# First adaLN modulation of a hybrid encoder layer: two of its four sum blocks made by one-row TensorE products, x's squares shared by ScalarE and VectorE, and the first token half's products written ahead

## Chip, cores and metric

The kernel runs on one core of a Trainium2 chip. Its time is the device time of one execution in microseconds (us). A run of it takes about 1318 us, and its executions lie within 0.3% of each other. TensorE (PE in the profile) multiplies matrices into PSUM; VectorE (DVE), ScalarE (ACT) and GpSimd (POOL) work on tiles element by element; SyncE (SP) issues all transfers. Every engine works off its own list of instructions in order, and the engines wait for each other by semaphores.

## The reference, cut to what matters

The layer is a residual block of two sub-layers. The change lies in the first lines:

```python
mod = jnp.dot(jax.nn.silu(c), w_ada[l]) + b_ada[l]          # c: (1, 1024), w_ada: (1024, 6*1024)
sh_a, sc_a, g_a, sh_m, sc_m, g_m = jnp.split(mod, N_MOD, axis=-1)
h = modulate(rmsnorm(x, g_attn_norm[l]), sh_a, sc_a)        # rmsnorm(x)*g*(1+sc_a) + sh_a, x: (1, 1024, 1024)
proj = jnp.dot(h, w_in[l])                                  # split into latents, rotary key and q, k, v
# two attentions (latent attention, chunked band attention), output projection, gated residual,
# then a second modulated norm, a gated MLP with a causal convolution, gated residual
```

Only `sh_a` and `sc_a` (two times 1024 numbers, each a sum over 1024 rows of `w_ada`) and the squares of `rmsnorm(x)` are computed in another way by the change. The results are the same but for rounding.

## The kernel before, in words

All data is float32. A product that needs full accuracy is made of three products of rounded parts (`gemm3`, L154 to L156: high by high, high by low, low by high). `x` is held as eight blocks of 128 tokens (`x0` to `x7`, in the listing of instructions x_112 to x_126 by even numbers), and the 1024 channels as eight groups d of 128. Tokens come in two halves h of 512.

The first stage (up to about 70 us) goes so:

- **Squares.** For each block of x, ScalarE squares it and sums it along the row (L224), GpSimd turns the sum into 1/sqrt(mean) by two small operations (L119, L120), and VectorE scales the block by it (L226).
- **Modulation sums.** `w_ada` for shift and scale comes as four blocks dd of 512 columns (two channel groups d each), each in four transfers of 512 KB (`adaw`, L209) with five buffers for all of them. `ada_pair(dd)` sums a block: VectorE multiplies the eight 128-row slices by one column of silu(c) each and adds them up in `adacc` (L276 for the first, L278 for the other seven). That leaves 128 partial sums for each column, and TensorE adds them over the partitions by multiplying with ones (`p_ada`, L293). Three small VectorE operations (L296 to L298) make the scale and the shift of channel group d, `modT`.
- **Pages.** For each d and h, TensorE transposes four blocks of x (`ht_ps`, L233, one PSUM bank for each h), and `mod_transpose` applies scale and shift. The rounded high part `hT` is written by ScalarE (L236). The exact value `hv` is written by ScalarE for h = 0 (L239) and VectorE for h = 1 (L241). The low part is the difference, made by GpSimd for h = 0 and VectorE for h = 1 (both L242).
- **Products.** For each d, 24 products of 256 columns add to the first query and key projection `qk` (eight token blocks, three products each). After d = 7 ScalarE reads the sums (L349), and the next projection (`ipv`) and the first attention follow.
- **Weights.** The first value projection's weights (`wv_r`, eight transfers of L258, issued behind the last `adaw`) are split while d = 4 to 7 are worked on: high part by VectorE (L81), low part by GpSimd (L84), squares by VectorE (L267).

The loop over d calls `ada_pair(dd + 1)` at each even d ahead of its own pages, so VectorE's sums for the next block are written between the pages of this one. The order in which instructions stand on each engine is not that of the code alone: a scheduler that runs over the whole program places each instruction where it expects it to become ready. Transfers are all issued by SyncE in one list; a transfer into a buffer that is still read holds up those behind it.

After the first stage come the band attention (to about 340 us), the latent attention (to about 600 us), the output projection and the MLP (to the end).

Of the kernel before, what the change touches and what calls it, by code (L numbers as in the profile page):

```python
# [13 lines left out]
F32 = mybir.dt.float32  # L14
# [50 lines left out]
def layer_kernel(ctx, tc, I, out):  # L65
# [155 lines left out]
    for t in range(NT):  # L221
        xt = xs[t]
        junk = st.tile([P, D], mybir.dt.bfloat16, name=f"xj{t}", tag="hv", bufs=2)
        act.activation(junk[:], xt[:], AF.Square, accum_out=ssx[:, t:t + 1])  # L224
        rsqrt_mean(rx[:, t:t + 1], ssx[:, t:t + 1], D)
        dve.tensor_scalar(xt[:], xt[:], rx[:, t:t + 1], None, op0=MUL)  # L226
# [34 lines left out]
    def wv0_split(k):  # L261
        w = hw.tile([P, 2, 256], F32R, name=f"wv0_s{k}", tag="ws", bufs=16)
        junk = st.tile([P, 512], F32, name=f"wv0_j{k}", tag="wvj", bufs=1)
        with tc.issue_after(anchor["lov"]), tc.issue_after(anchor["lop"]):
            hi_of("v", w[:, 0], wv0r[k][:])
            lo_of("p", w[:, 1], wv0r[k][:], w[:, 0])
            dve.tensor_tensor_reduce(junk[:, :256], wv0r[k][:], wv0r[k][:], 1.0, 0.0, MUL, ADD,  # L267
                                     accum_out=ssw0[:, k:k + 1])
        wv0.append((w[:, 0], w[:, 1]))

    def ada_pair(dd):
        acc = rtile(f"adacc_{dd}")
        for k in range(ND):
# [5 lines left out]
        accs[dd] = acc  # L279

    ada_pair(0)
    for d in range(ND):
        dd, half = divmod(d, 2)
        if half == 0 and dd + 1 < ND // 2:
            for c in range(4):
                load_ada(dd + 1, c)
            if dd + 2 == ND // 2:
                wv0_load()
            ada_pair(dd + 1)
        pt = ps.tile([P, 512], F32, name=f"p_ada{d}", tag="mm", bufs=2)  # L290
        for i in range(2):
            c0 = half * 256 + i * P
            pe.matmul(pt[:, i:i + 1], accs[dd][:, c0:c0 + P], ones[:, 0:1], start=True, stop=True)  # L293

# [3 lines left out]
        dve.tensor_tensor(modT[:, 1, d:d + 1], pt[:, 1:2], pk[:, C_B + d:C_B + d + 1], op=ADD)  # L298
        for h in range(2):
            hT[d, h] = mod_transpose(lambda j: xs[4 * h + j][:, d * P:(d + 1) * P], d, h, 0, ps, ("T", "pv")[h], 1,  # L300
                                     hw, "hT", st, 16, "v" if h else "a", "v" if h else "p")
# [3 lines left out]
        for t in range(NT):  # L305
            h, j = divmod(t, 4)
            sl = slice(j * P, (j + 1) * P)
            gemm3(qk0[h][:, j * 256:(j + 1) * 256],
                  [(hT[d, h][:, 0, sl], hT[d, h][:, 1, sl]) + wqk[d]], start=(d == 0 and j % 2 == 0), stop=(d == ND - 1 and j % 2 == 1))
# [1350 lines left out]
```

## Time and profile before

| | |
|---|---|
| median of three runs | 1318.42 us (1316.21 to 1319.64) |
| the profiled execution | 1320.49 us, its span 1318.7 us |
| mean granted TensorE clock | 0.964 |
| busy: PE, DVE, ACT, POOL | 1192.2, 1080.2, 627.3, 597.4 us |
| instructions | 18701 |

The page has a line for each engine's busy time and the span in 40 slices. The views used below are the timeline (start, duration, engine, line, operation, and in brackets the idle time before it and what ended it), tables of busy time in chosen stretches, the waits in a stretch, and the instructions of one line or tile. A duration of a pipelined TensorE product is longer than the step to the next one.

### The profile page before, as it was taken

The numbers are of one execution on the slowest core, as the hardware profiler recorded it, in microseconds if no ns is written. First come the engines' busy times: TensorE is split into PE (matmuls) and PEld (weight loads), VectorE is DVE, ScalarE is ACT, GpSimd is POOL, SyncE is SP. The second block draws the span as 40 slices with busy tenths as digits, with TensorE's granted clock in tenths as the row PEclk, the third lists the DMA queues.
The fourth block names the chain that finished last, engine by engine and source line by source line (L and its number), as shares of the span: only waits on it lengthen the run. The fifth ranks groups of instructions, "written<-read, shape, count | busy, mean of one in ns | idle before, by whom it ended". The sixth has DMA issues, their size and how long they took to land. (4 is left out here: it accounts for less than half of the span.)

```text
span 1318.7 us, 18701 instructions
## 1 busy us (share of the span) xinstructions
PE 1192.2 (90%) x6168; PEld 993.5 (75%) x6168; DVE 1080.2 (82%) x1864; ACT 627.3 (48%) x1148; POOL 597.4 (45%) x629
## 2 busy tenths in 40 slices
PE   4899889988768987868899999999999999999998
PEld 3789889878546766756777888888888886888886
DVE  6979988887589988874789888888889887687667
ACT  5455654455656454542375444443444444433331
POOL 5485773586687643454616444554444431000000
PEclk9999898989879899989999999999999999999999
DMA  8416768665233687789602334333343337943441
GB/s 326 144 55 153 170 146 187 157 161 119 48 85 62 148 165 155 146 173 300 265 17 84 125 104 136 112 114 125 93 131 106 128 104 245 394 145 109 128 160 64
DMA packets 223690, 190.83 MB, mean 145 GB/s; under 512 B 148709, under 2 KB 166373, under 8 KB 223593
## 3 DMA queue, kind: packets, MB, share of 16 engines
q1 hardware_dynamic: 223592, 189.64, 50.5%
q8 instruction: 48, 0.79, 0.2%
q14 instruction: 50, 0.40, 0.1%
HBM read 117.50 MB, written 37.49 MB: 118 GB/s over the span
## 5 line engine op out<-in xcount | busy, mean ns | idle before, releaser
L77 ACT ACTIVATE dnP<-dnr 128x1024 fp32r<-128x1024 f32 x73 | 77.5, 1064 | 116.1 <-PE dnA_P L1471 46.4
L1443 DVE TENSOR_TENSOR dnP<-dnr,dnP 128x1024 fp32r<-128x1024 f32 x72 | 88.7, 1236 | 51.8 <-ACT dnP L77 51.7
L73 POOL TENSOR_SCALAR hlm<-Pm,rim 128x512 f16<-128x512 f32 (+3 forms) x96 | 67.9, 716 | 66.7 <-issue 22.5
L84 POOL TENSOR_TENSOR wf<-wu,wf 128x512 fp32r<-128x512 f32 x22 | 38.6, 1752 | 116.6 <-ACT wf L77 116.6
L84 POOL TENSOR_TENSOR wb<-wu,wb 128x512 fp32r<-128x512 f32 x22 | 44.9, 2040 | 84.5 <-ACT wb L77 56.9
L1305 DVE SCALAR_TENSOR_TENSOR u<-c,cvp,u 128x1023 f32<-128x1023 f32 x44 | 55.8, 1310 | 27.6 <-ACT u L1304 24.8
L855 DVE SCALAR_TENSOR_TENSOR hlm<-Pm,rim,hlm 128x512 f16<-128x512 f32 (+3 forms) x96 | 68.7, 728 | 6.4 <-POOL hlm L73 6.2
L73 POOL TENSOR_SCALAR hlc<-Pc,ric 128x640 f16<-128x640 f32 (+2 forms) x64 | 49.7, 780 | 47.3 <-DVE ric L836 18.4
L833 ACT ACTIVATE Pc<-sc,mc 128x640 f32<-128x640 f32 (+2 forms) x64 | 42.3, 661 | 54.3 <-DVE mc L822 37.2
L833 ACT ACTIVATE Pm<-sm,mm 128x128 f32<-128x128 f32 (+3 forms) x64 | 47.2, 737 | 37.3 <-DVE mm L826 20.0
L895 PE MATMUL pvm<-PTm,vt 128*128 128x256 f16 (+1 forms) x320 | 43.6, 284 | 22.6 <-DMA PTm<-hlm 21.6
L1304 ACT ACTIVATE u<-c,cvp 128x1024 f32<-128x1024 f32 x44 | 52.4, 1238 | 23.6 <-DVE c L1403 16.7
L895 PEld LDWEIGHTS <-vt 128*128 128x128 f16 x320 | 31.3, 105 | 35.9 <-DMA PTm<-hlm 15.8
L855 DVE SCALAR_TENSOR_TENSOR hlc<-Pc,ric,hlc 128x640 f16<-128x640 f32 (+2 forms) x64 | 51.3, 806 | 8.4 <-POOL hlc L73 8.2
L77 ACT ACTIVATE wc<-ws 128x512 fp32r<-128x512 f32 x21 | 13.3, 632 | 93.1 <-DVE ws L1153 87.2
L154 PE MATMUL ipq<-wq_s,hT 128*128 128x256 f32 x192 | 56.4, 294 | 0.0
L1306 DVE SCALAR_TENSOR_TENSOR u<-c,cvp,u 128x1022 f32<-128x1022 f32 x44 | 55.5, 1301 | 0.0
L155 PE MATMUL ipq<-wq_s,hT 128*128 128x256 f32 x192 | 55.0, 287 | 0.0
L156 PE MATMUL ipq<-wq_s,hT 128*128 128x256 f32 x192 | 55.0, 287 | 0.0
L1470 PE MATMUL dnA_P<-dnP 128*128 128x512 f32 x132 | 51.3, 389 | 0.0
L1471 PE MATMUL dnA_P<-dnP 128*128 128x512 f32 x132 | 51.3, 389 | 0.0
L1469 PE MATMUL dnA_P<-dnP 128*128 128x512 f32 x132 | 51.2, 389 | 0.0
(441 smaller groups left out, 4420.5 us busy)
## 6 DMA issues: line engine op xcount, KB each, us to landing
wu<-w_up SPq DMA_DIRECT2D x44, 512.0 KB, 3.6
dnr<-g_d SPq DMA_DIRECT2D x73, 256.0 KB, 2.7
aw<-w_ada SPq DMA_DIRECT2D x48, 256.0 KB, 3.2
g_d<-u SPq DMA_DIRECT2D x22, 512.0 KB, 3.0
dnr<-w_down SPq DMA_DIRECT2D x44, 256.0 KB, 5.4
adaw<-w_ada_a SPq DMA_DIRECT2D x16, 512.0 KB, 6.2
x<-x SPq DMA_DIRECT2D x16, 512.0 KB, 9.4
g_d<-gs SPq DMA_DIRECT2D x22, 256.0 KB, 2.8
```

Of the source, the lines that this page charges most:

```text
L73: pool.tensor_scalar(o, i, s, 1.0, op0=MUL, op1=MUL)
L77: act.activation(o, i, AF.Copy)
L84: (pool if eng == "p" else dve).tensor_tensor(o, i, f32(hi), op=SUB)
L154: pe.matmul(pt, sh, mh, start=(start and i == 0), stop=False)
L155: pe.matmul(pt, sh, ml, start=False, stop=False)
L156: last = pe.matmul(pt, sl, mh, start=False, stop=(stop and i == n - 1))
L833: act.activation(pr[:, :n], sv, AF.Exp, bias=m[:], scale=-1.0, accum_out=rsum[:, 0:1])
L855: dve.scalar_tensor_tensor(hl[:, w:2 * w], pp, ri[:], hl[:, :w], op0=MUL, op1=SUB)
L895: last = pe.matmul(dst, u.vst(j), mov, start=(x == 0), stop=(x == len(todo) - 1), skip_group_check=True)
L1305: dve.scalar_tensor_tensor(u[:, 1:], c[:, :S - 1], cvp[:, cv + 1:cv + 2], u[:, 1:], op0=MUL, op1=ADD)
L1306: dve.scalar_tensor_tensor(u[:, 2:], c[:, :S - 2], cvp[:, cv:cv + 1], u[:, 2:], op0=MUL, op1=ADD)
L1443: r = f(*a, **k)
```

## The change

Three things are rewritten.

1. `ada_pair` for blocks 0 and 1 makes no VectorE sums. Eight plain float32 products with one column of silu(c) as the stationary side and a 128x512 slice of `w_ada` as the moving side add up to a single row of 512 sums in PSUM (`p_row`). ScalarE copies the row to `adacc` (one partition). The `p_ada` products then take that one row instead of 128 rows. Blocks 2 and 3 are summed by VectorE as before.
2. The squares of x1, x3, x5 and x7 are made by VectorE (`tensor_tensor_reduce`), those of the even blocks by ScalarE as before. The high parts of the value weights (`wv_s`) are made by ScalarE, not by VectorE.
3. The loop is unrolled for d = 0 and 1: the pages and products of token half 0 stand first, then block 1's sums, then half 1's pages and products. The PSUM bank of a page is taken in turn ("T", "pv"), no longer by its half. From d = 2 on the loop is as before.

```diff
-        act.activation(junk[:], xt[:], AF.Square, accum_out=ssx[:, t:t + 1])
+        if t % 2:
+            dve.tensor_tensor_reduce(junk[:], xt[:], xt[:], 1.0, 0.0, MUL, ADD, accum_out=ssx[:, t:t + 1])
+        else:
+            act.activation(junk[:], xt[:], AF.Square, accum_out=ssx[:, t:t + 1])
...
-            hi_of("v", w[:, 0], wv0r[k][:])
+            hi_of("a", w[:, 0], wv0r[k][:])
...
     def ada_pair(dd):
         acc = rtile(f"adacc_{dd}")
+        if dd in (0, 1):
+            pr = ps.tile([P, 512], F32, name=f"p_row{dd}", tag="mm", bufs=2)
+            for k in range(ND):
+                pe.matmul(pr[0:1, :], cs[:, k:k + 1], wada[dd, k // 2][:, k % 2], start=(k == 0), stop=(k == ND - 1))
+            act.activation(acc[0:1, :], pr[0:1, :], AF.Copy)
+            accs[dd] = acc[0:1, :]
+            return
         for k in range(ND):
             w = wada[dd, k // 2][:, k % 2]
             if k == 0:
                 dve.tensor_scalar(acc[:], w, cs[:, 0:1], None, op0=MUL)
             else:
                 dve.scalar_tensor_tensor(acc[:], w, cs[:, k:k + 1], acc[:], op0=MUL, op1=ADD)
...
+    def mod_cols(d):
...
-            pe.matmul(pt[:, i:i + 1], accs[dd][:, c0:c0 + P], ones[:, 0:1], start=True, stop=True)
+            src = accs[dd][:, c0:c0 + P]
+            pe.matmul(pt[:, i:i + 1], src, ones[:src.shape[0], 0:1], start=True, stop=True)
...
+    def mod_page(d, h):
+        tag = ("T", "pv")[nht[0] % 2]
...
+    ada_pair(0)
+    mod_cols(0)
+    mod_cols(1)
+    for d in range(2):
+        mod_page(d, 0)
+        qk_part(d, 0)
+    ada_next(1)
+    for d in range(2):
+        mod_page(d, 1)
+        qk_part(d, 1)
+    for d in range(2, ND):
+        dd, half = divmod(d, 2)
+        if half == 0 and dd + 1 < ND // 2:
+            ada_next(dd + 1)
+        mod_cols(d)
         for h in range(2):
-            hT[d, h] = mod_transpose(lambda j: xs[4 * h + j][:, d * P:(d + 1) * P], d, h, 0, ps, ("T", "pv")[h], 1,
-                                     hw, "hT", st, 16, "v" if h else "a", "v" if h else "p")
+            mod_page(d, h)
         if d >= ND // 2:
             for k in range(2 * d - ND, 2 * d - ND + 2):
                 wv0_split(k)
...
+        for h in range(2):
+            qk_part(d, h)
```

(`mod_cols` holds the `p_ada` products and the three small operations, `qk_part` the twelve products of one d and half, `ada_next` the four transfers of a block, behind the last of them the value weights' transfers, and `ada_pair`.)

What the scheduler makes of it is seen in three places. The first is VectorE's list behind the scaling of the last blocks of x. Before (adacc_228 is block 1's sum, hv_0_1 and hT_0_1 the page of d = 0, h = 1):

```order
L226 TENSOR_SCALAR x_124<-x_124,rx 128x1024
L226 TENSOR_SCALAR x_126<-x_126,rx 128x1024
L276 TENSOR_SCALAR adacc_228<-adaw_0_220,cs 128x512
L278 SCALAR_TENSOR_TENSOR adacc_228<-adaw_0_220,cs,adacc_228 128x512
L278 SCALAR_TENSOR_TENSOR adacc_228<-adaw_1_222,cs,adacc_228 128x512
L241 TENSOR_SCALAR hv_0_1_261<-ht_ps_0_1_254,modT 128x512
L278 SCALAR_TENSOR_TENSOR adacc_228<-adaw_1_222,cs,adacc_228 128x512
L242 TENSOR_TENSOR hT_0_1_259<-hv_0_1_261,hT_0_1_259 128x512
```

And now (adacc_351 is block 2's sum, p_ada_360 and p_ada_411 are the products of d = 2 and 3, which need block 1's row):

```order
L225 ISA xj_163,ssx<-x_126 128x1024
L225 ISA ssx 128x1
L229 TENSOR_SCALAR x_124<-x_124,rx 128x1024
L229 TENSOR_SCALAR x_126<-x_126,rx 128x1024
L286 TENSOR_SCALAR adacc_351<-adaw_0_343,cs 128x512
L288 SCALAR_TENSOR_TENSOR adacc_351<-adaw_0_343,cs,adacc_351 128x512
L299 TENSOR_SCALAR adat_363<-p_ada_360,pk 128x1
L301 TENSOR_TENSOR modT<-p_ada_360,pk 128x1
L244 TENSOR_SCALAR hv_0_1_306<-ht_ps_0_1_299,modT 128x512
L288 SCALAR_TENSOR_TENSOR adacc_351<-adaw_1_345,cs,adacc_351 128x512
L300 TENSOR_TENSOR modT<-adat_363,pk 128x1
```

Block 1's eight sums are gone from here, and after two of block 2's sums an operation stands that reads block 1's products (`adat`); the first page of half 1 stands behind it.

The second place is TensorE's list ahead of those products. Before:

```order
L233 MATMUL ht_ps_2_1_373<-ident,x_126 128x128
L293 MATMUL p_ada_356<-ones,adacc_228 128x1 x2
L293 MATMUL p_ada_407<-ones,adacc_228 128x1 x2
L156 MATMUL qk_1_209<-wq_s_173,hT_1_1_310 128x256
L154 MATMUL qk_1_209<-wq_s_173,hT_1_1_310 128x256
```

And now:

```order
L156 MATMUL qk_0_208<-wq_s_173,hT_1_0_263 128x256
L279 MATMUL p_row_289<-adaw_2_284,cs 1x512
L279 MATMUL p_row_289<-adaw_3_286,cs 1x512 x2
L236 MATMUL ht_ps_0_1_299<-ident,x_126 128x128
L236 MATMUL ht_ps_1_1_321<-ident,x_126 128x128
L297 MATMUL p_ada_360<-ones,adacc_288 128x1 x2
L297 MATMUL p_ada_411<-ones,adacc_288 128x1 x2
L154 MATMUL qk_1_209<-wq_s_168,hT_0_1_304 128x256
```

Before, 38 of the 48 products of d = 0 and 1 and all transposes of d = 2 stand ahead of `p_ada` for d = 2; now half 0's 24 products of d = 0 and 1 and block 1's eight row products stand there, and half 1's 24 products come behind.

The third place is ScalarE's list ahead of the first page of d = 4 (hT_4_0). Before:

```order
L236 ACTIVATE hT_3_0_419<-ht_ps_3_0_414,modT 128x512
L239 ACTIVATE hv_3_0_421<-ht_ps_3_0_414,modT 128x512
L77 ACTIVATE wq_s_203<-wq_r_0_204 128x256
L236 ACTIVATE hT_3_1_429<-ht_ps_3_1_424,modT 128x512
L236 ACTIVATE hT_4_0_503<-ht_ps_4_0_498,modT 128x512
```

And now:

```order
L242 ACTIVATE hv_3_0_425<-ht_ps_3_0_418,modT 128x512
L77 ACTIVATE wv_s_522<-wv_r_470 128x256
L77 ACTIVATE wv_s_527<-wv_r_472 128x256
L77 ACTIVATE wv_s_583<-wv_r_474 128x256
L239 ACTIVATE hT_3_1_433<-ht_ps_3_1_428,modT 128x512
L77 ACTIVATE wv_s_588<-wv_r_476 128x256
L77 ACTIVATE wv_s_644<-wv_r_478 128x256
L77 ACTIVATE wv_s_649<-wv_r_480 128x256
L77 ACTIVATE wv_s_705<-wv_r_482 128x256
L77 ACTIVATE wv_s_710<-wv_r_484 128x256
L239 ACTIVATE hT_4_0_507<-ht_ps_4_0_502,modT 128x512
```

All eight high parts of the value weights, and with them the landing of their eight transfers, now stand ahead of the first page of d = 4. From there to the first latent products (`mp`, about 260 us) the order of every engine is the same in both kernels; between about 290 and 600 us some products, transposes and pages change places with their neighbours, because the scheduler's own estimate of the start has moved.

31 lines of the change are left out of this document (17 added, 14 removed).

## The prediction

> **What bounds the kernel now.** I read the table of busy time by stretch for the first 70 us first (columns: PE, PE's weight loads, DVE, ACT, POOL, granted clock, DMA share, GB/s), then the waits, then the timeline of VectorE and TensorE.
>
> ```profile
> 12.00:25.40 13.40, 6.22 (x20) 4.12 (x20) 7.59 (x14) 10.64 (x21) 10.83 (x18) 1.00 1.02 404
> 25.40:32.00 6.60, 6.32 (x29) 6.02 (x30) 6.49 (x9) 3.30 (x6) 4.45 (x5) 1.00 0.74 239
> 32.00:42.00 10.00, 7.12 (x50) 5.75 (x48) 9.89 (x19) 3.67 (x7) 4.54 (x4) 1.00 0.81 275
> 42.00:46.00 4.00, 3.65 (x19) 3.65 (x20) 4.00 (x4) 1.21 (x4) 3.60 (x4) 0.57 0.95 268
> 46.00:54.80 8.80, 7.71 (x63) 7.26 (x62) 8.77 (x23) 4.38 (x6) 2.25 (x2) 1.00 0.43 135
> 54.80:70.70 15.90, 13.76 (x112) 12.91 (x111) 15.76 (x41) 5.80 (x9) 9.70 (x11) 1.00 0.01 2
> ```
>
> Up to 25.4 the stage runs at the pace at which x arrives and is normalised. From 25.4 to 70.7 VectorE has hardly a gap (6.49 of 6.60, 9.89 of 10.00, 15.76 of 15.90), while PE leaves 6.7 of 45.3 us open. The wait that shows the price is ScalarE's for the modulation:
>
> ```profile
> ACT hT L236 <- DVE modT L297: 9.8, 2, 6.3
> ```
>
> ```profile
> 22.30 0.75 DVE L226 TENSOR_SCALAR x<-x,rx 128x1024 f32<-128x1024 f32 x1 [0.71 <-POOL rx L120]
> 25.44 0.94 DVE L276 TENSOR_SCALAR adacc<-adaw,cs 128x512 f32<-128x512 f32 x1
> 37.67 0.20 DVE L296 TENSOR_SCALAR adat<-p_ada,pk 128x1 f32<-128x1 f32 x1
> 50.13 0.78 ACT L236 ACTIVATE hT<-ht_ps,modT 128x512 fp32r<-128x512 f32 x1 [3.43 <-DVE modT L297]
> 67.42 1.59 DVE L242 TENSOR_TENSOR hT<-hv,hT 128x512 fp32r<-128x512 f32 x1
> 70.02 1.09 ACT L349 ACTIVATE raw<-qk 128x512 f32<-128x512 f32 x2 [4.18 <-PE qk L156]
> ```
>
> These are the milestones: x6 scaled by 23.05, block 1's sums from 25.44, `adat` for d = 2 at 37.67, the first page of d = 4 at 50.13, VectorE's last low part at 69.0, the stage's end at 70.02. What follows is bound by PE and VectorE, and the order of every engine up to 260 us is unchanged, so I take a shift of 70.02 to reach the end of the kernel one to one.
>
> **Block 0's row products.** Nothing like them is in the trace; the nearest are the gate's plain float32 products of the same 512 columns, with all 128 stationary columns:
>
> ```profile
> 140.44 2.05 PE L486 MATMUL p_ada<-aacc,ones 128*128 128x512 f32 x2
> 171.31 1.02 PE L486 MATMUL p_ada<-aacc,ones 128*128 128x512 f32 x2
> ```
>
> ```profile
> 26.54 0.42 PE L156 MATMUL qk<-wq_s,hT 128*128 128x256 f32 x1
> 26.76 0.42 PE L154 MATMUL qk<-wq_s,hT 128*128 128x256 f32 x1
> 29.53 1.91 PE L233 MATMUL ht_ps<-ident,x 128*128 128x128 f32 x8
> 31.86 0.28 PE L156 MATMUL qk<-wq_s,hT 128*128 128x256 f32 x1
> 31.98 0.28 PE L154 MATMUL qk<-wq_s,hT 128*128 128x256 f32 x1
> ```
>
> One product is two records, 1.02 us at full clock, of which the next covers 0.16 (a projection product lasts 0.28 and steps 0.12): 0.86. At half clock (step 0.22) it is twice that, 1.7, at most 2.05. Bounds for eight: 6.9 and 16.4 us. One stationary column instead of 128 could make it cheaper only if the pace were set by the weights; the time here goes with the 512 moving columns, so I stay with these.
>
> ```profile
> 5.86 0.49 DVE L276 TENSOR_SCALAR adacc<-adaw,cs 128x512 f32<-128x512 f32 x1 [2.69 <-DMA adaw<-w_ada_a]
> 13.94 1.06 ACT L224 ACTIVATE xj<-x 128x1024 bf16<-128x1024 f32 x1 [0.20 <-DMA x<-x]
> 12.55 0.19 POOL L119 TENSOR_SCALAR ssx<-ssx 128x1 f32<-128x1 f32 x1 [11.12 <-ACT xj L224]
> 16.48 0.75 POOL L119 TENSOR_SCALAR ssx<-ssx 128x1 f32<-128x1 f32 x1
> 17.32 0.55 POOL L120 TENSOR_TENSOR rx<-ssx,nhalf 128x1 f32<-128x1 f32 x1
> 56.06 0.41 DVE L267 CUSTOM_DVE_ANT_0 wv_j<-wv_r 128x256 f32<-128x256 f32 x1
> 24.93 3.18 POOL L84 TENSOR_TENSOR wq_s<-wq_r,wq_s 128x256 fp32r<-128x256 f32 x3
> ```
>
> The first slice is there at 5.86. In the rows above the clock needed some 5.5 us of dense products (from about 26.2 to 31.8) to rise. With 5.5 us at half clock (3.2 products) and 4.8 products at 0.86, the row is done at 15.5; all at half clock it is 19.5. [...]
>
> **The chain of x.** The row's copy (0.55, half of the pair at 70.02) stands in ScalarE's list ahead of x2's square, which starts at 16.1 instead of 13.94: 2.2 us later, and with it the even blocks. x3's square on VectorE stands behind `adat` of d = 0, so it too waits for the row. Such a square of 1024 columns costs between a scaling (0.75) and four of the 0.41 us squares (1.64); I take 1.2. GpSimd's small operation takes 0.19 alone and 0.75 beside a scaling. If it is held off by VectorE's squares as well, x2, x3, x4, x5, x6 are scaled by 20.0, 21.6, 24.1, 25.7, 28.2; if not, x6 is scaled by 25.9. I take 27, 4 us later than before. [...]
>
> **Block 1's row.** PE takes it up behind x6's transposes, at about 27.3. Ahead of `adat` for d = 2 stand 24 projection products and 8 row products, 24 × 0.12 + 8 × 0.86 = 9.8 us at full clock. The transposes before leave PE mostly idle, so I count the clock as low again and the first 5.5 us at half: 2.75 more, 39.8. Copy and `p_ada` add 1.1, so `adat` comes at 41.0 (39.9 to 42.2) instead of 37.67. VectorE has only two of block 2's sums between x7's scaling (27, two low parts of 1.3 and three weight splits of GpSimd's, 3.18, that now stand ahead of it: 33) and this `adat`, so it stands still for 5 us or more: the eight sums taken off it come back as a wait.
>
> **From there to d = 4.** Rows for VectorE's steps:
>
> ```profile
> 34.36 0.80 DVE L241 TENSOR_SCALAR hv<-ht_ps,modT 128x512 f32<-128x512 f32 x1
> 35.08 1.40 DVE L278 SCALAR_TENSOR_TENSOR adacc<-adaw,cs,adacc 128x512 f32<-128x512 f32 x2
> 36.40 0.68 DVE L242 TENSOR_TENSOR hT<-hv,hT 128x512 fp32r<-128x512 f32 x1
> 37.01 0.74 DVE L278 SCALAR_TENSOR_TENSOR adacc<-adaw,cs,adacc 128x512 f32<-128x512 f32 x1
> 40.79 6.37 SPq L258 DMA_DIRECT2D wv_r<-w_v  x8
> wv_r<-w_v SPq DMA_DIRECT2D x16, 128.0 KB, 4.6
> ```
>
> From start to start a page value is 0.72, a sum 0.66, a low part 0.61. Between `adat` and the scale of d = 4 now stand 13 sums (8.6), a first sum (0.45), four page values (2.9), four low parts (2.4) and small ones and the bias (1.4): 15.8 us, with 1.7 for GpSimd's low parts 17.5, against 12.4 before (37.67 to 50.1). That gives 58.5. The second gate is the value weights: their eight casts now stand in ScalarE's list ahead of d = 4's first page. Their transfers wait for block 3's last one, and that for a buffer that VectorE frees some 9 us behind `adat`, at about 50; 6.4 us of issue and the median landing of 4.6 make 61 at most, less if they don't queue behind others as in these rows. I take 59 for the page, 8.9 later than 50.13.
>
> **The tail.** Before, the stage took 19.9 us from that page, all of it VectorE's. Now VectorE has no casts and no sums left there, and PE sets the pace: 96 products × 0.12 = 11.5, and six groups of transposes:
>
> ```profile
> 35.87 1.05 PE L293 MATMUL p_ada<-ones,adacc 128*128 128x1 f32 x8
> 55.05 0.60 PE L233 MATMUL ht_ps<-ident,x 128*128 128x128 f32 x4
> 55.40 0.36 PE L154 MATMUL qk<-wq_s,hT 128*128 128x256 f32 x1
> ```
>
> 0.35 to 0.45 each, 2.5; the page itself 0.8 and the wait for its low part 1.3: 16.1, so the end is at 75.1. **Sum: 8.9 − (19.9 − 16.1) = +5.1 us**, with the bounds above from +2.8 to +8.
>
> **The middle.** Between 290 and 600 us neighbours change places. The size of what hangs on that:
>
> ```profile
>   DMA PTm<-hlm: 21.6, 15
> ```
>
> Fifteen waits of PE for transposed scores, 1.4 us each: two of them opened or closed are ±3 us, with no reason for a sign. I count 0 and keep ±3 for the range.
>
> The profiled execution took 1320.49, its span 1318.7, the median of the runs 1318.42. The shift of 5 us holds for each; on the median it gives 1323.5.
>
> **Rivals.** A measurement of this kernel tells about 0.3%, 4 us, from no change. *Faster* (0.12): the clock, raised by block 0's row, holds through the transposes, and x6 is scaled by 25.9. Then block 1's row and half 0's products take 9.8 us from 26.4 and end at 36.2, `adat` comes before 37.67, and PE's own work is the bound: 168 products (20.2), 12 groups of transposes (4.8), `p_ada` (three times 1.05): 64.3, 5.7 us less than 70.02, 1312.7. For it speaks that 8 × 0.66 us of sums and eight casts leave the engine that has no gap; against it that PE is busy less than half of 12 to 25.4 (6.22 of 13.40). It decides at one point: the page of d = 2 is written before 39. [...] *No change* (0.26): clock or port are kinder by half, `adat` comes at 39, the transfers land by 57, and the end is at 72 to 73; 1320.5. *Slower by more* (0.14): one-column products do not raise the clock. The first row ends at 19.5, x and everything behind it is 4 us later: +9, 1327.5. The forecast, +4 to +7, gets 0.48.
>
> So slower by over 0.3% has 0.62, within it 0.26, faster 0.12. The range reaches from the lower part of "no change" to the half-clock case with the middle's 3 us: 1317 to 1330.
>
> **What would show it.** Right: `adat` for d = 2 at 40 to 42 with an idle time of VectorE of 5 us or more put down to PE; block 0's row done at 15 to 16; x6 scaled at 26 to 28; the page of d = 4 behind a wait at 57 to 61; the read of `qk` at 73 to 78; the rest shifted as it stands. Wrong: row products of 0.5 us or less each; `adat` before 38; `qk` read before 70; or a difference that only begins behind 290 us.

## The result, and the profile after

The changed kernel takes 1329.26 us (median, 1325.04 to 1332.13) against 1318.42 us. Its ratio to the kernel before is 1.0072 (95% interval 1.0047 to 1.0097). Executed again beside other kernels it gave 1330.16 us and 1.0077 (1.0055 to 1.0098). So it is slower by some 11 us, about twice the 5.1 us forecast; its median lies inside the range (1317 to 1330), less than 1 us from its upper end. Single executions differ by more than the 0.3% named at the start: in a later series the kernel before ranged from 1312.17 to 1326.92 over 20 executions. Medians and intervals are compared below, not single times.

The profiled execution took 1325.04 us, the shortest of its five, with a span of 1323.3 us and a mean granted clock of 0.959. In the changed kernel the scaling of x is L229, `adat` L299, the page L239 and the read of `qk` L386. The timelines of VectorE and ScalarE, after (start, duration, engine, line, operation, and in brackets the idle time ahead of it with what ended it):

```profile
26.42 1.74 DVE L229 TENSOR_SCALAR x<-x,rx 128x1024 f32<-128x1024 f32 x1 [0.43 <-POOL rx L120]
32.27 1.21 DVE L229 TENSOR_SCALAR x<-x,rx 128x1024 f32<-128x1024 f32 x1 [4.11 <-POOL rx L120]
41.98 0.57 ACT L280 ACTIVATE adacc<-p_row 1x512 f32<-1x512 f32 x1
43.25 0.22 DVE L299 TENSOR_SCALAR adat<-p_ada,pk 128x1 f32<-128x1 f32 x1 [7.74 <-PE p_ada L297]
61.69 0.78 ACT L239 ACTIVATE hT<-ht_ps,modT 128x512 fp32r<-128x512 f32 x1 [3.14 <-DVE modT L300]
78.04 1.09 ACT L386 ACTIVATE raw<-qk 128x512 f32<-128x512 f32 x2 [1.62 <-PE qk L156]
```

VectorE stands still for 7.74 us ahead of the `adat` of d = 2, waiting for PE. The first page of d = 4 comes at 61.69 instead of 50.13, and the read of `qk` at 78.04 instead of 70.02. The first stage is 8.0 us longer.

PE's rows of the two row sums, after:

```profile
6.56 8.59 PE L279 MATMUL p_row<-adaw,cs 128*1 128x512 f32 x16 [6.56 <-DMA adaw<-w_ada_a]
29.26 3.57 PE L279 MATMUL p_row<-adaw,cs 128*1 128x512 f32 x4
34.89 2.73 PE L279 MATMUL p_row<-adaw,cs 128*1 128x512 f32 x6
38.94 2.73 PE L279 MATMUL p_row<-adaw,cs 128*1 128x512 f32 x6
42.61 1.05 PE L297 MATMUL p_ada<-ones,adacc 1*128 1x1 f32 x8 [0.56 <-ACT adacc L280]
```

Two records are one product. Block 0's row took 8.59 us and was done at 15.15. Block 1's row took 9.0 us of PE in three pieces between 29.26 and 41.67, with the projection products between them. The busy time by stretch, after (columns: PE, PE's weight loads, DVE, ACT, POOL, granted clock, DMA share, GB/s):

```profile
25.40:32.00 6.60, 4.25 (x11) 1.22 (x9) 2.32 (x3) 1.61 (x4) 6.43 (x8) 0.50 0.38 138
32.00:43.20 11.20, 10.64 (x44) 4.88 (x43) 3.20 (x3) 2.72 (x7) 4.35 (x6) 0.93 0.57 176
43.20:61.70 18.50, 14.34 (x110) 12.79 (x110) 17.75 (x38) 7.85 (x17) 3.22 (x3) 1.00 0.64 202
61.70:78.00 16.30, 15.94 (x118) 15.29 (x118) 15.22 (x30) 8.56 (x12) 12.95 (x14) 0.90 0.01 2
```

Before, VectorE was busy for 6.49 of 6.60 us and 9.89 of 10.00 us from 25.4 to 42. Now it works 5.5 of 17.8 us from 25.4 to 43.2, while PE works 10.64 of 11.20. From 25.4 to 32 GpSimd is the full engine (6.43 of 6.60): VectorE waits 4.11 us for it ahead of x7's scaling. From 32 to 43.2 the bound is PE. From 43.2 to 61.7 VectorE has no room again (17.75 of 18.50).

Not all of the 8.0 us reaches the end in this execution. The output projection regained 6.2 us: its products took 54.0 us before (598.8 to 652.8) and 47.8 after (608.3 to 656.1), mostly because a wait shrank from 5.6 to 1.0 us. PE's waits from 596 us on, of before (first fence) and of after (second):

```profile
PE op L156 <- POOL ol L84: 5.6, 2, 4.9
```

```profile
PE op L156 <- POOL ol L84: 1.0, 2, 0.6
```

### The profile page after: what moved, and what is told of

It reads as the page before. It is cut to its first block, busy times and chain, and to the rows that moved or that the text cites. A ratio compares the mean times of both kernels' runs of the same rounds, so it can differ in the third digit from the quotient of the medians.

```text
span 1323.3 us, 18740 instructions
## 1 busy us (share of the span) xinstructions
PE 1206.3 (91%) x6200; PEld 991.8 (75%) x6200; DVE 1087.4 (82%) x1848; ACT 623.6 (47%) x1150; POOL 579.9 (44%) x629
## 5 line engine op out<-in xcount | busy, mean ns | idle before, releaser
L73 POOL TENSOR_SCALAR hlm<-Pm,rim 128x512 f16<-128x512 f32 (+3 forms) x96 | 64.4, 680 | 84.4 <-DVE rim L873 33.9
L1342 DVE SCALAR_TENSOR_TENSOR u<-c,cvp,u 128x1023 f32<-128x1023 f32 x44 | 70.2, 1634 | 27.6 <-ACT u L1341 27.6
L1343 DVE SCALAR_TENSOR_TENSOR u<-c,cvp,u 128x1022 f32<-128x1022 f32 x44 | 70.0, 1627 | 0.0
L870 ACT ACTIVATE Pc<-sc,mc 128x640 f32<-128x640 f32 (+2 forms) x64 | 42.2, 660 | 53.7 <-DVE mc L859 32.5
L932 PEld LDWEIGHTS <-vt 128*128 128x128 f16 x320 | 30.8, 106 | 35.6 <-issue 15.5
L84 POOL TENSOR_TENSOR wb<-wu,wb 128x512 fp32r<-128x512 f32 x22 | 34.4, 1562 | 49.2 <-ACT wb L77 49.2
```

Of the source, the lines that this page charges most:

```text
L73: pool.tensor_scalar(o, i, s, 1.0, op0=MUL, op1=MUL)
L84: (pool if eng == "p" else dve).tensor_tensor(o, i, f32(hi), op=SUB)
L870: act.activation(pr[:, :n], sv, AF.Exp, bias=m[:], scale=-1.0, accum_out=rsum[:, 0:1])
L932: last = pe.matmul(dst, u.vst(j), mov, start=(x == 0), stop=(x == len(todo) - 1), skip_group_check=True)
L1342: dve.scalar_tensor_tensor(u[:, 1:], c[:, :S - 1], cvp[:, cv + 1:cv + 2], u[:, 1:], op0=MUL, op1=ADD)
L1343: dve.scalar_tensor_tensor(u[:, 2:], c[:, :S - 2], cvp[:, cv:cv + 1], u[:, 2:], op0=MUL, op1=ADD)
```

## Experiments

Twelve more runs were made. The theory (A) was that block 1's row on PE's list is what makes the first stage late. The rivals were the later chain of x (B), the casts on ScalarE (C), the new loop order, and the clock. For each kernel the table gives the read of `qk`, the profiled execution's span less that time ("behind"), the median, the ratio to the kernel before, and the "excess": what the median lies above that of the kernel before, less what the read of `qk` lies behind 70.02. The kernel before was run again beside each group of runs; its medians were 1318.42 (changed), 1319.13 (u1 to u4), 1320.02 (u5 to u8) and 1318.96 (u9 to u12).

| kernel | read of `qk` | behind | median | ratio (95%) | excess |
|---|---|---|---|---|---|
| before | 70.02 | 1248.7 | 1318.42 | 1 | 0 |
| changed | 78.04 | 1245.3 | 1329.26 | 1.0072 (1.0047 to 1.0097) | 2.8 |
| u1 block 1 by VectorE | 73.35 | 1252.8 | 1324.17 | 1.0054 (1.0037 to 1.0072) | 1.7 |
| u2 squares on ScalarE | 76.30 | 1248.4 | 1325.69 | 1.0047 (1.0030 to 1.0065) | 0.3 |
| u3 casts on VectorE | 81.82 | 1257.4 | 1338.91 | 1.0152 (1.0110 to 1.0194) | 8.0 |
| u4 old loop order | 74.92 | 1260.2 | 1338.66 | 1.0152 (1.0122 to 1.0182) | 14.6 |
| u5 rows alone | 72.91 | 1256.1 | 1331.04 | 1.0083 (1.0055 to 1.0110) | 8.1 |
| u6 casts alone | 68.32 | 1251.2 | 1323.21 | 1.0025 (1.0006 to 1.0043) | 4.9 |
| u7 casts and order | 69.42 | 1247.0 | 1323.79 | 1.0029 (1.0009 to 1.0050) | 4.4 |
| u8 row 0, squares, casts | 73.45 | 1256.4 | 1329.51 | 1.0068 (1.0043 to 1.0092) | 6.1 |
| u9 half of block 1's row | 73.80 | 1251.9 | 1327.91 | 1.0059 (1.0038 to 1.0081) | 5.2 |
| u10 clock kept up | 79.54 | 1247.5 | 1329.06 | 1.0084 (1.0054 to 1.0114) | 0.6 |
| u11 changed, again | 80.81 | 1245.6 | 1330.16 | 1.0077 (1.0055 to 1.0098) | 0.4 |
| u12 two casts alone | 70.58 | 1248.0 | 1320.00 | 0.9997 (0.9976 to 1.0018) | 0.5 |

The start of a trace varies by some 0.5 us (the first row product starts at 6.37 to 6.92). The read of one kernel varies by more: the two profiles of the changed kernel (changed, u11) have 78.04 and 80.81. Every other kernel was profiled once, so a difference of reads under 3 us is weak by itself.

### u1 to u4: one part undone

**u1.** Block 1 by VectorE:

```diff
-        if dd in (0, 1):
+        if dd == 0:
```

> The changed kernel with one part undone: block 1 is summed by VectorE again; block 0's row, the squares in turn, the casts on ScalarE and the new loop order stay. Theory A (VectorE stands idle for block 1's row, which PE computes behind its products at 43.25): the eight sums, 8 x 0.66 us, fit in the idle time of 4.1 and 7.7 us that VectorE has there now, the modulation of d = 2 comes at 37 to 39 instead of 43.25, the read of qk at 71 to 74 instead of 78.04, the time 5 us under the changed kernel's median, 1323 to 1325. Theory B (the chain of x is late because of the squares on VectorE): x6 is still scaled at 28, the modulation of d = 2 comes at 41 to 43 and the read of qk at 76 to 78; time within 2 us of 1329. Theory C (the casts in ScalarE's list hold d = 4's pages): the modulation of d = 2 is earlier, but the read of qk stays at 76 to 78.

The timeline of VectorE and of ScalarE, u1:

```profile
41.52 0.20 DVE L299 TENSOR_SCALAR adat<-p_ada,pk 128x1 f32<-128x1 f32 x1
73.35 1.09 ACT L386 ACTIVATE raw<-qk 128x512 f32<-128x512 f32 x2 [1.62 <-PE qk L156]
```

And the busy time of one stretch, u1:

```profile
25.40:43.20 17.80, 13.17 (x56) 11.49 (x56) 16.31 (x24) 3.51 (x8) 11.13 (x11) 0.50 0.62 194
```

The wait for PE is gone and the stage ends 4.7 us earlier than in the changed kernel, as A has it. `adat` itself came later than A said (41.5, not 37 to 39): VectorE does the eight sums, two page values and a low part first. It is earlier by only 1.7 us, yet the stage by 4.7. What differs by then is the work that VectorE has behind it: it is busy for 16.31 of the 17.80 us to 43.2, in the changed kernel for 5.52. PE's clock is at half all through this stretch (0.50), so the gain doesn't come from the clock.

**u2.** Squares on ScalarE:

```diff
-        if t % 2:
+        if t < 0:
```

> The changed kernel with one part undone: all eight squares of x on ScalarE again; both rows, the casts and the loop order stay. Theory A: x6 is scaled some 3 to 4 us earlier (24 to 25 instead of 28.16), PE begins block 1's row so much earlier but at a low clock, the modulation of d = 2 comes at 39 to 41 with VectorE still idle for 6 us or more in front of it, the read of qk at 74 to 76, the time 1325 to 1327. Theory B: the squares carry the whole loss, the read of qk is back at 70 to 71 and the time at 1319 to 1321. Theory C (casts): read of qk at 77 or later.

The timeline of VectorE and of ScalarE, u2:

```profile
25.84 1.20 DVE L229 TENSOR_SCALAR x<-x,rx 128x1024 f32<-128x1024 f32 x1 [0.71 <-POOL rx L120]
44.49 0.48 DVE L286 TENSOR_SCALAR adacc<-adaw,cs 128x512 f32<-128x512 f32 x1 [6.96 <-DMA adaw<-w_ada_a]
44.89 0.21 DVE L299 TENSOR_SCALAR adat<-p_ada,pk 128x1 f32<-128x1 f32 x1
76.30 1.09 ACT L386 ACTIVATE raw<-qk 128x512 f32<-128x512 f32 x2 [2.09 <-PE qk L156]
```

x7 is scaled at 25.84 instead of 32.27, yet the read of `qk` is only 1.7 us earlier. B as the whole cause is out. A's steps are not met either: `adat` is later (44.89, not 39 to 41). PE has the products for it done by 42, but ahead of `adat` in VectorE's list stands a sum of the next block that waits 6.96 us for its transfer. So a block's transfer can stand on the path in PE's place. Only A's size for the end (74 to 76) is nearly right, and its time (1325 to 1327) is met.

**u3.** Casts on VectorE:

```diff
-            hi_of("a", w[:, 0], wv0r[k][:])
+            hi_of("v", w[:, 0], wv0r[k][:])
```

> The changed kernel with one part undone: the eight high parts of the value weights on VectorE again; rows, squares and loop order stay. Theory A: the page of d = 4 was gated by VectorE's modulation and not by the casts, so it stays at 60 to 62; VectorE gets eight casts back, which PE's pace in the tail hides for the most part: read of qk at 78 to 81, time 1329 to 1332. Theory B: no change in either, 78, 1329. Theory C (the casts in ScalarE's list, behind late transfers, hold the pages): page of d = 4 at 57 to 59, read of qk at 74 to 76, time 1325 to 1327.

The timeline of ScalarE, u3:

```profile
64.34 0.78 ACT L239 ACTIVATE hT<-ht_ps,modT 128x512 fp32r<-128x512 f32 x1 [9.55 <-DVE modT L300]
81.82 1.09 ACT L386 ACTIVATE raw<-qk 128x512 f32<-128x512 f32 x2 [1.60 <-PE qk L156]
```

The stage gets 3.8 us longer than the first profile of the changed kernel and 1.0 longer than its second (u11), so moving the casts back gains nothing and C is out as a cause of loss. The page of d = 4 did not stay at 60 to 62: it waits 9.55 us for VectorE. The total lost 9.7 us in the medians, more than the stage, and is outside the 1329 to 1332 expected.

**u4.** The loop in the old order:

```diff
-    mod_cols(0)
-    mod_cols(1)
-    for d in range(2):
-        mod_page(d, 0)
-        qk_part(d, 0)
-    ada_next(1)
...
+    for d in range(ND):
+        dd, half = divmod(d, 2)
+        if half == 0 and dd + 1 < ND // 2:
+            ada_next(dd + 1)
+        mod_cols(d)
...
```

> The changed kernel with one part undone: the loop is written in the old order again (block 1's row ahead of the pages of d = 0, both token halves together); both rows, the squares and the casts stay. PE's list now has block 1's row within the last transposes of d = 0 and ahead of all projection products. Theory A: the modulation of d = 2 no longer waits behind 24 products; the row starts when its weights and x6 allow, 28, and takes 7 to 13 us at the granted clock: 37 to 41 instead of 43.25, idle time of VectorE in front of it under 4 us, read of qk at 73 to 76, time 1324 to 1327. Theory B (the chain of x decides): modulation of d = 2 and read of qk within 1 us of the changed kernel. Theory C (the row holds up the first pages and products instead): read of qk at 78 or later, time 1329 or more.

VectorE's and ScalarE's timeline, u4:

```profile
32.12 0.22 DVE L299 TENSOR_SCALAR adat<-p_ada,pk 128x1 f32<-128x1 f32 x1 [2.06 <-PE p_ada L297]
46.40 0.20 DVE L299 TENSOR_SCALAR adat<-p_ada,pk 128x1 f32<-128x1 f32 x1
74.92 1.08 ACT L377 ACTIVATE raw<-qk 128x512 f32<-128x512 f32 x2 [2.11 <-PE qk L156]
```

Now block 1's row holds up the modulations of d = 0 and 1 (32.12 and 39.93 instead of 16.70 and 18.11). The modulation of d = 2 comes at 46.40, not at A's 37 to 41 and 3.2 us later than in the changed kernel. Still the stage ends 3.1 us earlier, within A's 73 to 76. So `adat` of d = 2 alone doesn't set the end of the stage. The time is 9 us longer, as C has it, but not in the stage: 1260.2 us lie behind it.

### u5 to u8: one part alone, and kernels with the same order behind

A listing of the instructions shows that u6, u7 and u8 have one and the same order on every engine from the first PV product on, and that this order is not that of before. What the scheduler places differently at 300 to 600 us hangs on the first stage, but several first stages lead to the same order behind. The traces agree: behind 260 us PE, VectorE, ScalarE and GpSimd each have one sequence of operations in u6, u7 and u8, and that of before in u12. In u3, u4, u5 and, less, u10 the sequence differs from that of before even between the read of `qk` and the first latent products.

**u5** has only the first part of the change (rows), **u6** only the casts, **u7** casts and loop order, **u8** block 0's row, squares and casts:

```diff
 u5: before, with
+        if dd in (0, 1):
+            pr = ps.tile([P, 512], F32, name=f"p_row{dd}", tag="mm", bufs=2)
...
 u6: before, with
-            hi_of("v", w[:, 0], wv0r[k][:])
+            hi_of("a", w[:, 0], wv0r[k][:])
 u7: u6 in the new loop order
 u8: u6 with
+        if dd == 0:
+            pr = ps.tile([P, 512], F32, name=f"p_row{dd}", tag="mm", bufs=2)
...
+        if t % 2:
+            dve.tensor_tensor_reduce(junk[:], xt[:], xt[:], 1.0, 0.0, MUL, ADD, accum_out=ssx[:, t:t + 1])
```

> The kernel before with one part alone: both rows as products of PE; squares on ScalarE, casts on VectorE, the old loop order. Theory A (the rows cost the stage its time: PE computes block 1's row while VectorE waits): VectorE stands idle for 4 us or more in the stage and has its sums of blocks 2 and 3 and eight casts to do behind it; the read of qk at 75 to 79 instead of 70.02, the time 1324 to 1330, of which what the middle's order adds is not included. Theory B (squares and casts carry the loss): read of qk at 71 or earlier, time 1318 to 1320.

> The kernel before with one part alone: the eight high parts of the value weights on ScalarE; all sums on VectorE, squares on ScalarE, the old loop order. Theory A (VectorE has no gap from 25 to 70 and PE sets the pace only in the tail): the casts, median 0.81 us each, go from VectorE's list; the read of qk is at 66 to 68 instead of 70.02, and if a shift of the stage's end reaches the end of the kernel one to one, the time is 1314 to 1317 against 1318 to 1319. Theory C (the casts in ScalarE's list, behind late transfers, hold the pages): read of qk at 71 or later, time 1319 or more.

> The kernel before with two parts: casts on ScalarE and the new loop order (half 0's products ahead); no rows, squares on ScalarE. From the first PV product on, its order on every engine is the same as that of the casts alone, so the difference of the two times should be that of their reads of qk (one to one). Theory A: the order brings or costs at most 1.5 us as long as no row stands on PE's list: read of qk at 65 to 69, time within 2 us of the casts alone. Rival (the order itself is what costs, by holding half 1's pages): read of qk 3 us or more later than with the casts alone.

> The changed kernel with block 1's row and the loop order undone: block 0's row, the squares in turn and the casts stay. Its order from the first PV product on is the same as that of the casts alone. Theory A (block 0's row and the squares make x late, by some 4 us at x6; block 1's row adds the rest): the read of qk is 2.5 to 4.5 us later than with the casts alone, 69 to 72, and the time later by the same (one to one), 1317 to 1321. Rival (the end's shift is not passed on one to one): stage later by 2.5 us or more, time within 1 us of the casts alone.

The reads of `qk` of u6, u7 and u8, each from the timeline of ScalarE:

```profile
68.32 1.09 ACT L377 ACTIVATE raw<-qk 128x512 f32<-128x512 f32 x2 [2.88 <-PE qk L156]
```

```profile
69.42 1.09 ACT L386 ACTIVATE raw<-qk 128x512 f32<-128x512 f32 x2 [2.88 <-PE qk L156]
```

```profile
73.45 1.09 ACT L377 ACTIVATE raw<-qk 128x512 f32<-128x512 f32 x2 [1.62 <-PE qk L156]
```

Three things follow.

- **With one order behind, the shift goes through about one to one, in the medians.** From u6 to u7 the read moves by 1.1 us and the median by 0.6. From u6 to u8 they move by 5.1 and 6.3. The spans of the single profiled executions don't show it: 1251.2, 1247.0 and 1256.4 us lie behind the read, with one and the same order. Behind the stage a single execution thus varies by some 5 us to either side, and the column "behind" can't tell one order from another.
- **The excess tells the orders apart.** It is 4.4 to 6.1 us for the three kernels of one order, 0.5 for u12, which has the order of before, and 8.0 to 14.6 for u3, u4 and u5. So another order behind the stage is worth up to some 15 us, give or take 3 to 6 for the intervals and the reads. For the changed kernel it is 2.8 and 0.4, which is not clear of zero.
- **The casts shorten the stage by 1.7 us**, less than A's 2 to 4. The kernel is still slower, by 1.0025, and the 1314 to 1317 expected are missed (1323.21): the gain of the stage did not reach the end. The order that came with the casts is the likely reason; no run changed that order alone.
- **The loop order without a row costs 1.1 us** (u7 against u6), within A's 1.5; the read, 69.42, lies just past A's 65 to 69.
- **Block 0's row and the squares cost 5.1 us** (68.32 to 73.45), slightly more than the 2.5 to 4.5 expected; the time of u8, 1329.51, is far above the 1317 to 1321 expected, since those were counted from a faster u6. This needs no row for block 1. x7 is scaled at 32.10 in u8, and PE's clock is at half (0.50) from 24 into the stretch from 40 to 44. From the table of stretches, u8:

```profile
40.00:44.00 4.00, 4.00 (x24) 4.00 (x22) 3.33 (x6) 0.00 (x0) 0.04 (x1) 0.56 0.87 252
```

The rows alone (u5) lengthen the stage by 2.9 us, less than A's 5 to 9, and the kernel by 1.0083. Both rows without the squares thus cost less than block 0's row with them: what a part costs hangs on the others.

### u9, u10: block 1's row and the clock

**u9.** Half of block 1's row:

```diff
             for k in range(ND):
-                pe.matmul(pr[0:1, :], cs[:, k:k + 1], wada[dd, k // 2][:, k % 2], ...)
+                c = slice(0, 64) if dd and k in (1, 2, 5, 6) else slice(0, 512)
+                pe.matmul(pr[0:1, c], cs[:, k:k + 1], wada[dd, k // 2][:, k % 2, c], ...)
```

> The changed kernel with half of block 1's row: four of its eight products run on 64 columns instead of 512, so the sum lacks half its terms in the other 448 columns; everything else stays. Theory A (PE's time for block 1's row stands between the products and the modulation of d = 2): four products, 0.9 us each at the granted clock of that place, less four of some 0.15 us, 3 us, go from the path: the modulation of d = 2 at 39 to 41 instead of 43.25, the idle time of VectorE in front of it 4 to 6 instead of 7.74 us, the read of qk at 74 to 76 instead of 78.04. The time 1324 to 1328, since the order of the middle changes with it. Rival (what makes the stage late is the chain of x or the casts, and the row is hidden): the modulation of d = 2 and the read of qk within 1 us of the changed kernel.

The timeline of VectorE and of ScalarE, u9:

```profile
38.24 0.81 DVE L244 TENSOR_SCALAR hv<-ht_ps,modT 128x512 f32<-128x512 f32 x1 [5.08 <-ACT hT L239]
41.34 0.21 DVE L300 TENSOR_SCALAR adat<-p_ada,pk 128x1 f32<-128x1 f32 x1
73.80 1.09 ACT L387 ACTIVATE raw<-qk 128x512 f32<-128x512 f32 x2 [1.62 <-PE qk L156]
```

The stage ends 4.2 us earlier than in the first profile of the changed kernel and 7.0 earlier than in the second. The rival, a hidden row, is out: PE's row stands on the path. A said 2 to 4. `adat` comes 1.9 us earlier, just past A's 39 to 41. VectorE now has page values ahead of `adat` and waits 5.08 us for the page instead, so the idle time did not just shrink, it moved.

**u10.** Useless products between x and block 1's row, to hold the clock up:

```diff
         dve.tensor_scalar(xt[:], xt[:], rx[:, t:t + 1], None, op0=MUL)
+        if t in (4, 5):
+            for c in range(2):
+                pe.matmul(qk0[1][0:1, :512], cs[:, t:t + 1], xt[:, c * 512:(c + 1) * 512], start=True, stop=True)
```

> The changed kernel with four more one-row products of PE on the scaled x4 and x5, into a bank that is overwritten later: work without a use that keeps PE busy from 23 to 28, so that the clock is up when block 1's row begins. PE's list behind them is that of the changed kernel but for the place of block 1's products behind both d's of half 0. Theory A (with the clock's part): what PE does at half clock from 28.2 to 33.6 takes 2.7 us instead of 5.4; the modulation of d = 2 at 40 to 42 instead of 43.25, the read of qk at 75 to 77, the time 1325 to 1329. Rival 1 (the clock costs nothing there, the row waits for something else): both within 0.7 us of the changed kernel. Rival 2 (one-row products do not raise the clock once it has fallen): the first record of full clock no earlier than 33, the products themselves push the row 3 us back, modulation at 45 or later, read of qk at 80 or later.

Timelines of PE, VectorE and ScalarE, u10:

```profile
23.86 5.55 PE L233 MATMUL qk<-x,cs 128*1 128x512 f32 x8 [1.64 <-DVE x L230]
30.27 1.88 PE L282 MATMUL p_row<-adaw,cs 128*1 128x512 f32 x4
41.65 0.22 DVE L302 TENSOR_SCALAR adat<-p_ada,pk 128x1 f32<-128x1 f32 x1 [5.70 <-PE p_ada L300]
56.10 0.42 ACT L77 ACTIVATE wv_s<-wv_r 128x256 fp32r<-128x256 f32 x1 [5.95 <-DMA wv_r<-w_v]
61.73 0.78 ACT L243 ACTIVATE hT<-ht_ps,modT 128x512 fp32r<-128x512 f32 x1 [2.40 <-DVE modT L303]
79.54 1.09 ACT L389 ACTIVATE raw<-qk 128x512 f32<-128x512 f32 x2 [2.09 <-PE qk L156]
```

Busy time by stretch, u10:

```profile
28.00:32.00 4.00, 4.00 (x15) 1.14 (x13) 0.59 (x1) 0.42 (x1) 3.84 (x6) 1.00 0.20 62
64.00:68.00 4.00, 4.00 (x20) 4.00 (x21) 3.52 (x13) 1.45 (x2) 2.33 (x4) 0.50 0.02 4
```

The clock was up from 28 on, the first two products of the row took 1.88 instead of 3.57 us, and `adat` came 1.6 us earlier, all as A says. The end did not follow: 79.54, not A's 75 to 77. The page of d = 4 is where it was (61.73), most likely because the transfers of the value weights are late next (5.95 us of waiting in ScalarE's list, 4.29 in the changed kernel). From 60 to 68 us the clock was at half (0.50 over 60 to 64 and over 64 to 68), in the changed kernel for some 3.4 us (0.59 over 64 to 66, 0.56 over 66 to 68); from the page of d = 4 to the read passed 17.8 us, there 16.35. So the clock at 28 us costs 1.6 us of modulation. What it is worth at the end this run can't tell, since later transfers and a slower tail took the gain back.

### u11, u12: the changed kernel again, and the version that the runs point to

> The changed kernel itself, once more, beside the others. Theory A (the first stage's end is fixed, what comes behind it varies from run to run): the read of qk at 77.5 to 78.5 again, the time 1326 to 1331 in the median, the difference from the kernel before 8 us from the first stage and 0 to 3 from the stretch from 290 to 655, where PE waits for transfers. Rival (the stage's end varies from run to run as well): the read of qk 2 us or more from 78.04.

Timelines of VectorE and ScalarE, u11:

```profile
42.77 0.22 DVE L299 TENSOR_SCALAR adat<-p_ada,pk 128x1 f32<-128x1 f32 x1 [7.46 <-PE p_ada L297]
47.64 0.89 DVE L286 TENSOR_SCALAR adacc<-adaw,cs 128x512 f32<-128x512 f32 x1 [1.63 <-DMA adaw<-w_ada_a]
56.44 1.13 ACT L77 ACTIVATE wv_s<-wv_r 128x256 fp32r<-128x256 f32 x3 [5.63 <-DMA wv_r<-w_v]
63.26 0.78 ACT L239 ACTIVATE hT<-ht_ps,modT 128x512 fp32r<-128x512 f32 x1 [3.19 <-DVE modT L300]
80.81 1.09 ACT L386 ACTIVATE raw<-qk 128x512 f32<-128x512 f32 x2 [1.62 <-PE qk L156]
```

Busy time by stretch, of u11 and of the first profile of the changed kernel:

```profile
64.00:68.00 4.00, 4.00 (x20) 4.00 (x20) 3.42 (x10) 2.49 (x5) 2.66 (x3) 0.50 0.00 0
68.00:72.00 4.00, 4.00 (x25) 4.00 (x25) 3.93 (x7) 1.61 (x3) 3.29 (x3) 0.63 0.01 4
```

```profile
64.00:68.00 4.00, 3.82 (x19) 3.61 (x20) 3.93 (x6) 1.33 (x2) 4.00 (x5) 0.57 0.01 4
```

And the rows of that first profile for the same two waits on transfers, from its timelines:

```profile
46.93 0.48 DVE L286 TENSOR_SCALAR adacc<-adaw,cs 128x512 f32<-128x512 f32 x1 [0.44 <-DMA adaw<-w_ada_a]
55.05 1.18 ACT L77 ACTIVATE wv_s<-wv_r 128x256 fp32r<-128x256 f32 x3 [4.29 <-DMA wv_r<-w_v]
```

The same kernel, with an `adat` 0.5 us earlier, ends its first stage 2.8 us later. The rival of this run holds: the stage's end varies. The transfers land later (1.63 us of waiting for `adaw` where the first profile has 0.44, then 5.63 for the value weights where it has 4.29), and PE, which has waited meanwhile, runs at half clock over most of 61 to 71 us, where the first profile has it for some 3.4 us. Behind the stage both profiles have the same 1245 us. The time, 1330.16, is within A's 1326 to 1331.

**u12.** Two casts only, with exactly the order of before behind the stage:

```diff
-            hi_of("v", w[:, 0], wv0r[k][:])
+            hi_of("a" if k in (6, 7) else "v", w[:, 0], wv0r[k][:])
```

> The kernel before with the last two of the eight casts on ScalarE, nothing else; the order of every engine behind the first stage is exactly that of the kernel before. The version that the runs so far point to: a shorter first stage without another order behind it. Theory A: two casts of some 0.8 us leave VectorE's list ahead of its last low part; the read of qk at 68.3 to 69.3 instead of 70.02, the time 1 us less, 0.9985 to 1.0 of the kernel before, at the edge of what can be told. Rival (the end of the stage hangs on PE alone): the read of qk within 0.3 us of 70.02.

The timeline of ScalarE, u12:

```profile
50.70 0.78 ACT L239 ACTIVATE hT<-ht_ps,modT 128x512 fp32r<-128x512 f32 x1 [3.19 <-DVE modT L300]
70.58 1.09 ACT L377 ACTIVATE raw<-qk 128x512 f32<-128x512 f32 x2 [4.16 <-PE qk L156]
```

No gain: 0.9997 (0.9976 to 1.0018). From the first page of d = 4 to the read of `qk` pass 19.88 us, before 19.89 (50.13 to 70.02): taking the last two casts from VectorE does not shorten the tail. All eight do (50.08 to 68.32 in u6, 18.24). No version was found that beats the kernel before.

## Why the prediction held, and where it was off

**The direction and the mechanism held; the size did not, and that the median fell into the range is in part luck.** The forecast sum for the stage was +5.1 us; the two profiles have +8.0 and +10.8. Of the signs named for being right, block 0's row and VectorE's wait came as said. Four others came just past their late ends: x6 scaled (26 to 28) at 28.16, `adat` (40 to 42) at 43.25, the page of d = 4 (57 to 61) at 61.69, the read of `qk` (73 to 78) at 78.04, and in the second profile at 80.81. The range held the result because it reached up to the half-clock case and 3 us more. None of the signs for being wrong came.

**What is shown of the cause.** The eight sums taken off VectorE came back as a wait of 7.74 us (forecast: 5 or more) for PE's row. Taking the row away, whole (u1) or half (u9), takes back 4.7 and 4.2 us of the stage's 8.0, in the second profile's terms 7.5 and 7.0 of 10.8. The runs lead from before to the changed kernel by one part at a time: the casts −1.7 (u6), block 0's row with the squares +5.1 (u8), the loop order −0.1 (u1), block 1's row +4.7. That they sum to 8.0 is no check, since each starts where the last one ends. Another path gives other parts: with the old loop order block 1's row costs only 1.5 us (u4 against u8), and with both rows the new loop order costs 3.1 (changed against u4). So it is the row together with the new order that costs, as the prediction has it: in that order the row stands behind 24 products and ahead of `adat`.

**What is not.** That a later `adat` of d = 2 by itself makes the end later, step by step as the sum was built, does not hold from kernel to kernel: u4 and u2 have it at 46.40 and 44.89 and end earlier (74.92, 76.30), u10 has it at 41.65 and ends later (79.54). Transfers, the order on VectorE and the clock in the tail come in between.

**Step by step, in the first profile.** The sum was short by 2.9 us: `adat` 2.25, the page 0.4, the tail 0.25. In the second profile it was short by 5.7: 1.8, 2.5 and 1.4.

- *Block 0's row*: done at 15.15 (15.5 forecast). The price was right too: three products took 2.73 us and two 1.88 (u10), so one more costs 0.85 at full clock, where 0.86 was counted, and at half some 1.7 (3.57 for two). The rival that one-column products do not raise the clock is out, since eight at half clock would take over 13 us and not 8.59. (The column of the clock can't show when it rose here: in each trace it reads 1.00 up to the first change recorded, as in the table of before up to 32 us, where products at 26.5 still step by the 0.22 us of half clock.)
- *The chain of x*: x6 was scaled at 28.16, the late bound (28.2), where I took 27. This agreement is in part chance. The scaling began at 26.42, and with its usual 0.75 us it would have ended at 27.2; it took 1.74, beside a subtraction of GpSimd that began just ahead of it and that no term had. GpSimd's small operations took longer beside VectorE's squares, as they do beside its scalings (L119, after: 0.19 us at 28.83 with VectorE idle, 0.75 at 22.67 beside the scaling from 22.62 to 23.37). Its timeline, after, has two small operations of the same kind, the first alone, the second beside the square that VectorE makes from 24.76 to 25.98, and then that subtraction:

```profile
23.50 0.55 POOL L120 TENSOR_TENSOR rx<-ssx,nhalf 128x1 f32<-128x1 f32 x1
24.97 1.41 POOL L120 TENSOR_TENSOR rx<-ssx,nhalf 128x1 f32<-128x1 f32 x1
26.35 1.26 POOL L245 TENSOR_TENSOR hT<-hv,hT 128x512 fp32r<-128x512 f32 x1
```

  0.55 becomes 1.41 us. The "port" that the prediction's "no change" names is this slowing; the runs show its times, not its cause.
- *`adat` of d = 2*: 43.25 instead of 41.0, outside the bounds (39.9 to 42.2). The row and its projection products took 12.4 us (29.26 to 41.67), where 12.55 were worked out. They began 2 us late: 1.2 us are x6, and 0.8 its four transposes, which PE worked off first at half clock and which the sum had done by 27.3. Another 0.5 is the row's copy, which stood behind two casts in ScalarE's list.
- *The page of d = 4*: 61.69 instead of 59. From `adat` to the page 18.4 us passed where 18 were worked out, so here this step hands on the error of the one before it. In the second profile it is 20.5, with longer waits for transfers (u11).
- *The tail*: 16.35 us, where 16.1 were worked out, but as full clock all through. There were some 3.4 us of half clock in it (0.57 over 64 to 68), so other terms must have been too large: luck again. In the second profile the tail is 17.55, with half clock over some 7.7 us. Half clock in the tail was left out of the sum; before, the tail had none (1.00 from 54.8 on). In both profiles PE has gaps from 56 to 60 (busy for 2.80 and 2.58 of 4.00 us, before for 4.00); that this is why the clock fell is the author's guess and not shown.
- *One to one, the middle counted 0 with ±3 us*: this held, within what can be told. With one order the shift goes through (u6, u7, u8), and the changed kernel's excess is 2.8 and 0.4 us. But it was less safe than ±3: another order behind the stage, from a first stage not much different, is worth up to some 15 us (u4).

**What stays open.** In both profiles of the changed kernel the stretch behind the stage is 3 us shorter than before, so their spans are only 4.6 and 7.7 us longer, while the medians of the two series are 10.8 and 11.2 above those of the kernel before. The two profiles are among the shorter executions (1325.04 and 1328.16), and no profile shows one of 1332, so I can't say whether these lose the rest in the first stage's tail or at 300 to 650 us.

## What to carry to other kernels

Work moved from a full engine to one with gaps must be placed by what stands behind it in that engine's list: here PE had the time, but the products came between VectorE and its next input. PE, which waited more from 56 to 60, also ran a part of its later work at a lower clock here (0.57 over 64 to 68, before 1.00); whether the waiting is why, no run shows. Where a scheduler orders the whole program, an edit in one stage can change the order far behind it; compare the medians of kernels with the same order there before a difference of about 1% is put down to the edit. Parts that are undone one at a time need not add up: try them in more than one order.

## What the runs showed of the hardware

- A plain float32 product with one stationary column and 512 moving columns costs 0.85 to 0.86 us at full clock (2.73 for three in the changed kernel, 1.88 for two in u10), the same as one with 128 columns (0.86, worked out from the rows in the prediction).
- One-column products alone raised the clock in u10: PE did nothing but four of them from 23.86 to 29.3 us, and the clock was at 0.52 over 24 to 28 and at 1.00 over 28 to 32.
- The clock can stay at half while PE is busy without a gap. In u11 it was 0.50 over 64 to 68 with PE busy for 4.00 of 4.00, and 0.63 over 68 to 72. From 62 to nearly 71 us PE has no gap and the clock stays at half (0.50 in each us up to 70, 0.53 in the last). Elsewhere it rose sooner: in u10 after some 4 us of products, and of the 8.59 us of the changed kernel's first row some 3 were at half clock (an estimate from the 0.86 us that a product takes at full clock). No run shows what decides when it rises.
- An execution's first stage of the same program can end 2.8 us apart (78.04 and 80.81), with waits on transfers that are 1.2 and 1.3 us longer and a clock that stays low for longer (0.50 against 0.57 over 64 to 68, then 0.63).
